# A prefix log-sum-exp whose last store is cut into eight transfers

## The chip, the cores and the metric

The kernel runs on one core of a Trainium2 chip. The metric is the device time of one execution in microseconds. A core has five compute engines with a queue each (PE, the matrix engine; DVE, the vector engine; ACT, the scalar engine; POOL; SP, which here only issues transfers) and 16 DMA engines that move data between the chip's memory (HBM) and the core's own memory, SBUF, which has 128 partitions.

## The reference

For x of shape (4, 4096, 4128) in float32, each of the 4 x 4128 columns gets a running log-sum-exp along the 4096 rows:

```python
out[:, 0, :] = x[:, 0, :].copy()
for t in range(1, S):
    mx = np.maximum(out[:, t - 1, :], x[:, t, :])
    out[:, t, :] = mx + np.log(np.exp(out[:, t - 1, :] - mx) + np.exp(x[:, t, :] - mx))
```

This is the logarithm of the running sum of exp(x). Every byte is read once and written once: 270.53 MB in and 270.53 MB out.

## The kernel before, in words

The 4096 rows of a batch are cut into steps of 128 x r rows, r being 2 or 3 (lists `begin`, `usual`, `final`; 49 steps in all). Partition p of a step's tile `x` holds r neighbouring rows, r x 4128 values in a row, so partition p's part is one contiguous run in HBM of 33,024 B (r = 2) or 49,536 B (r = 3). Four tiles (slots) rotate.

A step is one load (`Step.load`, line 88), then three chunks of 1376 columns, then one store (`Step.store`, line 91). A chunk takes the exponentials in place on ACT (line 102), adds the rows of a partition on DVE (lines 114 and 116), sums over the partitions below with a triangular matrix on PE (line 124), adds that base on DVE (lines 133, and 141 or, in the last step of a batch, 136) and takes the logarithms on ACT (lines 146 and 147).

The order of each engine's work is written out by hand in lists: `moves` for the transfers, `act`, `vec` and `pe`. All loads and stores are issued from SP in the order of `moves`, one transfer for a whole tile: four loads first, then store, load, store, load; the end is load, load and then the stores alone. Each transfer signals one of eight landing counters, which are taken in turn (numbers 100, 101, 105 to 110 in the trace). Each DMA engine that takes part in a transfer signals it once its share has landed, so the trace has 16 landings for each of the 98 transfers.

The very last store (step 48: the last of the last batch, r = 2) is issued once its three chunks' logarithms are done. Behind it on SP stand the load of a flag that says whether the fast form of the sum was safe (line 254), a branch, and the closing waits for all landing counters (line 308). The span ends when these are through.

Of the kernel before, what the change touches and what calls it, by code (L numbers as in the profile page):

```python
# [12 lines left out]
P = 128  # L13
# [8 lines left out]
def kernel(  # L22
# [5 lines left out]
    nc = tc.nc  # L28
    B, S, D = x.shape
# [16 lines left out]
        out=below, in_=below, pattern=[[1, P]], compare_op=ALU.is_ge,  # L46
# [5 lines left out]
        out=carried, in_=below, pattern=[[0, P]], compare_op=ALU.not_equal,  # L52
# [25 lines left out]
    class Step:  # L78
# [9 lines left out]
            nc.sync.dma_start(out=self.xt, in_=self.dram(x))  # L88

        def store(self):  # L90
            nc.sync.dma_start(out=self.dram(out), in_=self.xt)  # L91

    class Chunk:
        def __init__(self, step, c):
# [125 lines left out]
    done, at = set(), {e: 0 for e in lists}  # L220
    while any(at[e] < len(l) for e, l in lists.items()):
        before = len(done), sum(at.values())
        for e, l in lists.items():
            while at[e] < len(l):
                op = l[at[e]]
                if op[1] < n:
# [3 lines left out]
                    of = steps[op[1]]  # L230
# [8 lines left out]
        out=fits[:, :B * NC], in0=probe, scalar1=LARGE, scalar2=None, op0=ALU.is_le,  # L239
    )  # L240
    nc.vector.tensor_scalar(
        out=fits[0:1, B * NC:], in0=short, scalar1=0.0, scalar2=None, op0=ALU.is_le,
# [7 lines left out]
        out=flag, in0=good, scalar1=float(P), scalar2=None, op0=ALU.is_lt,  # L250
# [62 lines left out]
```

## Time and profile before

| | |
|---|---|
| median of 3 runs | 1261.32 us (1260.91 to 1261.74) |
| profiled execution | 1260.2 us, of it span 1258.4 us |
| DVE, ACT, PE busy | 956.2, 955.4, 602.4 us |
| DMA | 14,131 packets, 541.28 MB, 430 GB/s on the mean |
| loads | 30 of 6192 KB, 19 of 4128 KB |
| stores | 30 of 6192 KB, 19 of 4128 KB |
| last store issued, last landing, end of span | 1239.89, 1257.13, 1258.4 us |

The span is the time from the first to the last instruction of the profiled execution; the execution's own time is 1.8 us longer. A packet is what one DMA engine moves in one go, here the part of one partition, or the 4 bytes that signal a landing. A landing is the moment at which the counter is raised. The trace gives a packet's size, start and duration, not the number of the DMA engine that moved it.

### The profile page before, as it was taken

How to read it: one execution, taken by the hardware profiler on the slowest of the kernel's cores; microseconds unless marked ns; L12 is line 12 of the kernel's file. 1: busy time of each engine (PE TensorE's matmuls, PEld its weight loads, DVE VectorE, ACT ScalarE, POOL GpSimd, SP SyncE). 2: the span in 40 equal slices, each digit the busy share in tenths (PEclk: the TensorE clock that was granted, in tenths of full speed). 3: DMA queues.
4: the chain of work that ended last, by engine and by line, in shares of the span. 5: the costliest groups of instructions: out<-in, count | busy, mean ns of one | idle time of the engine just before them, and what ended most of it. 6: DMA issues, size and time to landing. Idle time of an engine off the chain costs nothing.

```text
span 1258.4 us, 3228 instructions
## 1 busy us (share of the span) xinstructions
PE 602.4 (48%) x884; PEld 233.1 (19%) x884; DVE 956.2 (76%) x548; ACT 955.4 (76%) x466; POOL 4.6 (0%) x14
## 2 busy tenths in 40 slices
PE   3654454453535455345364535634535553463361
PEld 1221121121212122112121212211211211121120
DVE  3997696795967699579596679957957976795792
ACT  6987687786976699578697668866968966896792
POOL 1000000000000000000000000000000000000000
PEclk9877776676677667666676666766766776676676
DMA  9999999999999999999999999999999999999998
GB/s 403 420 439 426 432 436 428 432 437 429 439 425 438 430 437 433 436 435 427 440 422 436 436 432 434 434 430 435 437 428 437 431 435 431 434 437 433 432 435 354
DMA packets 14131, 541.28 MB, mean 430 GB/s; under 512 B 1568, under 2 KB 1568, under 8 KB 1568
## 3 DMA queue, kind: packets, MB, share of 16 engines
q1 hardware_dynamic: 14112, 541.07, 99.6%
q8 instruction: 7, 0.11, 0.0%
q14 instruction: 12, 0.10, 0.0%
HBM read 270.53 MB, written 270.53 MB: 430 GB/s over the span
## 4 chain that ended last, share of the span: by engine, by line
DMA 69%; ACT 14%; DVE 13%; PE 1%; issue 1%; SPq 0%; ACTq 0%; DVEq 0%
DMA x<-in_x_dram 52%; DMA out_dram<-x 17%; ACT x L102 6%; DVE x L133 5%; ACT x L146 5%; DVE z L116 3%; ACT x L147 3%; DVE z L141 3%; DVE x L114 2%; PE p L124 1%; SPq L91 0%; DVE z L136 0%; ACTq L146 0%; ACTq L254 0%; SPq L88 0%
## 5 line engine op out<-in xcount | busy, mean ns | idle before, releaser
L124 PE MATMUL p<-z,carried 128*128 128x512 f32 (+1 forms) x810 | 551.8, 842 | 544.3 <-DVE z L116 544.3
L102 ACT ACTIVATE x<-x 128x4128 f32<-128x4128 f32 (+1 forms) x147 | 468.0, 3187 | 219.7 <-DMA x<-in_x_dram 219.7
L124 PEld LDWEIGHTS p<-z,carried 128*128 128x128 f32 x810 | 213.4, 280 | 882.2 <-DVE z L116 648.3
L133 DVE TENSOR_TENSOR x<-p,x 128x2752 f32<-128x2752 f32 (+1 forms) x147 | 361.9, 2462 | 6.2 <-PE p L124 6.2
L146 ACT ACTIVATE x<-x 128x2752 f32<-128x2752 f32 (+1 forms) x147 | 300.6, 2045 | 63.5 <-DVE z L141 58.5
L114 DVE TENSOR_TENSOR x<-x 128x1376 f32<-128x1376 f32 x90 | 142.9, 1588 | 216.5 <-ACT x L102 216.5
L116 DVE TENSOR_TENSOR z<-x 127x1376 f32<-127x1376 f32 x147 | 233.9, 1591 | 53.8 <-ACT x L102 49.4
L141 DVE TENSOR_TENSOR z<-x 128x1376 f32<-128x1376 f32 x135 | 215.0, 1592 | 4.6
L147 ACT ACTIVATE x<-z 128x1376 f32<-128x1376 f32 x147 | 196.0, 1334 | 0.0
L124 PE MATMUL p<-z,below 128*128 128x512 f32 (+1 forms) x72 | 50.4, 864 | 87.4 <-DVE z L116 87.4
L124 PEld LDWEIGHTS p<-z,below 128*128 128x128 f32 x72 | 19.6, 289 | 117.7 <-DVE z L116 78.8
L136 DVE CUSTOM_DVE_ANT_0 z<-x 128x1376 f32<-128x1376 f32 x12 | 19.1, 1592 | 0.4
L105 ACT ACTIVATE spare<-x,tiny 1x1376 f32<-1x1376 f32 x12 | 17.3, 1442 | 0.5
L69 POOL MEMSET z<- 128x1376 f32 x3 | 3.7, 1241 | 0.0
L105 ACT ACTIVATION_READ_ACCUMULATOR spare<-x,tiny 1x1 f32 x12 | 2.2, 186 | 0.0
L247 PE MATMUL good<-ones,low 128*1 128x1 f32 x2 | 0.2, 164 | 3.8 <-DVE low L245 3.8
L34 ACT ACT_TABLE_LOAD x1 | 1.3, 1283 | 0.8 <-PEq L297 0.8
L136 DVE DVE_READ_ACCUMULATOR2_ANT probe<- 128x1 f32 x12 | 1.0, 83 | 0.0
L247 PEld LDWEIGHTS good<-ones,low 128*1 128x1 f32 x2 | 0.1, 80 | 4.8 <-DVE low L245 4.8
L249 DVE TENSOR_SCALAR flag<-good 1x1 int32<-1x1 f32 x1 | 0.1, 148 | 0.3 <-PE good L247 0.3
L51 POOL TENSOR_SCALAR_AFFINE_SELECT carried<-below 128x128 f32<-128x128 f32 x1 | 0.3, 290 | 0.0
L45 POOL TENSOR_SCALAR_AFFINE_SELECT below<-below 128x128 f32<-128x128 f32 x1 | 0.3, 285 | 0.0
(13 smaller groups left out, 1.6 us busy)
## 6 DMA issues: line engine op xcount, KB each, us to landing
x<-in_x_dram SPq DMA_DIRECT2D x30, 6192.0 KB, 38.4
out_dram<-x SPq DMA_DIRECT2D x30, 6192.0 KB, 25.0
x<-in_x_dram SPq DMA_DIRECT2D x19, 4128.0 KB, 33.0
out_dram<-x SPq DMA_DIRECT2D x19, 4128.0 KB, 21.6
```

The lines of the kernel that those rows point to most:

```text
L34: nc.scalar.preload_act_table_set("natural_log_exp_and_others")
L69: nc.gpsimd.memset(t, 0.0)
L102: nc.scalar.activation(e, e, ACT.Exp)
L105: nc.scalar.activation(spare, t.xt[0:1, 0, self.cols], ACT.Relu, bias=tiny, scale=-1.0, accum_out=short[:, k:k + 1],)
L114: nc.vector.tensor_tensor(out=e[1], in0=e[0], in1=e[1], op=ALU.add)
L116: nc.vector.tensor_tensor(out=self.z[0:n], in0=e[r - 2][0:n], in1=e[r - 1][0:n], op=ALU.add,)
L124: nc.tensor.matmul(pt[:, a:b], lhsT=w, rhs=self.z[:, a:b], start=True, stop=True,)
L133: nc.vector.tensor_tensor(out=e, in0=base, in1=e, op=ALU.add)
L136: nc.vector.tensor_tensor_reduce(out=self.z, in0=ends[0], in1=ends[1], scale=1.0, scalar=0.0, op0=ALU.add, op1=ALU.add, accum_out=probe[:, ...
L141: nc.vector.tensor_tensor(out=self.z, in0=ends[0], in1=ends[1], op=ALU.add)
L146: nc.scalar.activation(e, e, ACT.Ln)
L147: nc.scalar.activation(t.xt[:, r - 1, self.cols], self.z, ACT.Ln)
```

## The change

Every store but the last stays as it is. The last one is issued as eight transfers, in this order: the first 112 partitions in full; the last 16 partitions without their last 59 columns; then these 59 columns of the 16 partitions in three strips of 17, 19 and 23 columns, each strip as two transfers (14 and 2, 12 and 4, 10 and 6 partitions). The eight together write the same bytes to the same places.

```diff
         def store(self):
-            nc.sync.dma_start(out=self.dram(out), in_=self.xt)
+            if self.last and self.b == B - 1:
+                self.pieces()
+            else:
+                nc.sync.dma_start(out=self.dram(out), in_=self.xt)
+
+        def pieces(self):
+            to = self.dram(out).rearrange("p j d -> p (j d)")
+            of = self.xt.rearrange("p j d -> p (j d)")
+            a, end = P - 16, self.r * D
+            parts = [(2, 17), (4, 19), (6, 23)]
+            at = end - sum(w for _, w in parts)
+            nc.sync.dma_start(out=to[:a], in_=of[:a])
+            nc.sync.dma_start(out=to[a:, :at], in_=of[a:, :at])
+            for k, w in parts:
+                cols = slice(at, at + w)
+                at += w
+                nc.sync.dma_start(out=to[a:P - k, cols], in_=of[a:P - k, cols])
+                nc.sync.dma_start(out=to[P - k:, cols], in_=of[P - k:, cols])
+            assert at == end
```

## The prediction

> **What bounds the kernel now.** I read the page's slices first, then its queue part, and then only the end of the span, because the change touches only the last store.
>
> Part 2 and part 3 of the page (slices of the span; queues):
>
> ```profile
> DMA  9999999999999999999999999999999999999998
> GB/s 403 420 439 426 432 436 428 432 437 429 439 425 438 430 437 433 436 435 427 440 422 436 436 432 434 434 430 435 437 428 437 431 435 431 434 437 433 432 435 354
> q1 hardware_dynamic: 14112, 541.07, 99.6%
> ```
>
> The 16 DMA engines are busy from end to end, all of it on one queue, so a microsecond of compute is worth nothing and bytes per microsecond are everything. Only the last slice drops, to 354 GB/s: a tail. The windows of the last 20 us (columns: stretch, its length, five engines busy, granted clock, DMA share, GB/s) show it:
>
> ```profile
> 1240.00:1245.00 5.00, 0.00 (x0) 0.00 (x0) 0.00 (x0) 0.00 (x0) 0.00 (x0) 0.50 0.99 429
> 1245.00:1250.00 5.00, 0.00 (x0) 0.00 (x0) 0.00 (x0) 0.00 (x0) 0.00 (x0) 0.50 1.01 436
> ...
> 1251.00:1252.00 1.00, 0.00 (x0) 0.00 (x0) 0.00 (x0) 0.00 (x0) 0.00 (x0) 0.50 0.65 272
> 1252.00:1253.00 1.00, 0.00 (x0) 0.00 (x0) 0.00 (x0) 0.00 (x0) 0.00 (x0) 0.50 0.54 231
> 1253.00:1254.00 1.00, 0.00 (x0) 0.00 (x0) 0.00 (x0) 0.00 (x0) 0.00 (x0) 0.50 0.31 132
> 1254.00:1255.00 1.00, 0.00 (x0) 0.00 (x0) 0.00 (x0) 0.00 (x0) 0.00 (x0) 0.50 0.31 132
> ...
> 1256.00:1257.00 1.00, 0.00 (x0) 0.00 (x0) 0.00 (x0) 0.00 (x0) 0.00 (x0) 0.50 0.00 0
> ```
>
> No compute is left after 1240; the engines run out of packets one after another from 1251 on. The packet records say why. The last store is 128 packets of 33,024 B, eight per engine, each 1.222 us (least 1.221): 27.0 GB/s per engine, and 16 at once make the 432 of the windows. Its 16 landings (one per engine) are at 1251.55 to 1253.69 for eleven engines and 1256.07 to 1257.13 for five. The store before it has the same spread, 1241.77 to 1247.12, so 5.35 us of lateness was gathered earlier in the kernel. The last packet ends at 1256.67, and the last wait on SP, which ends with the final landing, is the longest of its line:
>
> ```profile
> SPq L308 <- DMA out_dram<-x: 15.4, 2, 10.0
> ```
>
> From that landing to the end of the span is 1.3 us of closing barriers. So the end is the latest engine: its eight packets, then about 1.75 us.
>
> The issuing side, from the timeline of SP and from line 91 (count: least/median/most ns, first and last start):
>
> ```profile
> 1188.24 0.34 SPq L88 DMA_DIRECT2D x<-in_x_dram  x1
> 1189.55 50.68 SPq L91 DMA_DIRECT2D out_dram<-x  x4
> ```
> ```profile
> L91 SPq DMA_DIRECT2D out_dram<-x x49: 332/332/347, 38.0 to 1239.9; - x49
> ```
>
> The last store is issued at 1239.89 and its first packet starts at 1241.38, when the queue gets to it.
>
> **The change, part by part.** One issue of 128 packets becomes eight issues of 112 + 16 + 14 + 2 + 12 + 4 + 10 + 6 = 176 packets. The bytes are the same.
>
> *Issuing.* Seven more issues on SP. The four loads that open the kernel are issued back to back at 0.80, 1.24, 1.71 and 2.18, so 0.47 us each: 7 x 0.47 = 3.3 us, the last at about 1243.2. The 16-partition store is needed when the earliest engine has done its seven packets, 1241.38 + 7 x 1.222 = 1249.9: covered by over 6 us. SP rotates eight landing counters. The last store uses 101, the new ones the next seven, the eighth piece that of the store issued at 1228.04, which lands at 1247.12. If SP waits for it, that piece goes out at 1247.2; from issue to first packet the opening load took 1.0 us (0.80 to 1.81): 1248.2, still before 1249.9. Behind that wait on SP stand the load of the flag and the branch (1240.28 to 1241.7, 1.4 us): done by 1249.1, and nobody needs SP before the landing at 1257. Cost 0; without the queue's backlog it would be the 3.3 us. POOL's queue is empty, and the closing waits already poll all eight counters, so no wait is added there.
>
> *Small transfers.* 48 packets of 68, 76 and 92 B, and seven more sets of landing writes (4 B, 0.009 us each). The 16 large last packets lose 236 B, 0.009 us. An engine has at most six small packets. Nothing of that size is in the trace: below, 0.009 us each, 0.05 us; above, each pair made to wait for its own write to land, by the last store's 0.46 us from packet end to landing (1256.67 to 1257.13), 6 x 0.46 = 2.8 us. I take 0.1, because landing writes in mid-stream hold up nothing: data packets follow them within 0.01 us. Below nothing is excluded: no byte goes away.
>
> *The new deal of partitions.* This is the term that matters. In every transfer of the trace 128 partitions go to 16 engines, eight each, in one fixed deal, so each engine always has the same eighth of partitions to itself. 112 and 16 partitions are dealt seven and one to an engine: still eight packets each, but now other partitions. If an engine's own 27.0 GB/s is the limit, the cost is 0. If the way out of SBUF for a group of eight partitions is the limit, also 27.0 GB/s, engines that meet in one group halve each other. The trace can't part the two, because no two engines ever share a group; the bounds come from the packet row.
> - The 16 last partitions: evenly spread over 16 ways, 0; all in two groups of eight, eight packets each where there was one, 7 x 1.222 = 8.56 us. I take four per way, 3 x 1.222 = 3.67, the whole number of packets closest to the middle (4.28).
> - The 112: at each of seven steps 16 engines read from at most 14 groups, so some double up. Least, 14 doublings shared by 16 engines, about one each, 1.22; most, the same pairs double at every step, 8.56 us. The engines are 5.35 us out of step, over four packets, so pairs form and dissolve: I take half of seven, rounded down, three, 3.67.
> A gain is bounded too: were the 16 dealt to early engines alone, the late five would be spared a packet, -1.22.
>
> The Trainium skill ("SBUF — State Buffer", section on the DMA port swizzle) speaks against the change: four neighbouring partitions and the four 32 further on share one of 16 ports, and a transfer over 16 partitions was measured there at 104 GB/s. By that rate the 16 partitions (524,608 B) would take an estimated 5.0 us where one packet time is 1.22, which makes that term +3.8 in place of 3.67. No run here shows it; the 27.0 GB/s per engine agrees with its 27.2 per port.
>
> Sum: 3.67 + 3.67 + 0.1 = +7.4 us. The profiled execution is 1260.2 us (span 1258.4 and 1.8 around it), 1.1 under the median of 1261.32, inside the habit of this kernel (1260.91 to 1261.74 timed). Profiled: 1267.6; median: 1268.7.
>
> **The rivals.** What a measurement of this kernel can tell from no change is about 0.2%, 2.5 us.
> - *No sharing*: the engine is the limit, and eight packets are eight packets wherever they come from. For it: 1.221 to 1.222 us in loads and stores alike, and an instruction fetch on the same engine just adds (1.53 = 1.222 + 0.309). Against: nothing, since the two limits have one value here. Time 1261.3 + 0.1 = 1261.4.
> - *Harder sharing*: the last 16 through two groups, +8.56, and the 112 at +6.1 (five of seven): 1276. It needs partitions grouped in plain runs of eight; but then a plain deal of eight is the only one that gives today's full rate.
> - *Serial small pieces*: no sharing, but each waits for its landing: +2.8, 1264.1. It counts only if the six-piece engines are among the late five; an early engine has up to 5.35 us to spare.
> - *Faster*: the lateness itself shrinks. A longer instruction stream moves the fetches: the late stretch holds one of 16,384 B at 1215.3 (0.89 us) and two of 8,192 B at 1205.5 and 1251.2 (0.31 each). If all three moved from late to early engines, -1.5, 1259.8; it decides only from 2.5 us, so two of the earlier large fetches (0.91 to 0.99 us each) must move too: 1257.9. The packet at 1251.51 that took 1.49 us shows that a fetch does hit the tail.
> - *Not what it says*: rows of 8,197 elements could be cut into more packets (8,197 = 7 x 1,171), 112 in place of 16; at 0.009 us a packet less than 0.1 us per engine. Price nil.
>
> **How the numbers follow.** Sharing as summed 0.62, no sharing 0.21 (1260.7 to 1262), harder sharing 0.08, serial pieces 0.05, faster 0.04. I lean to sharing because 16 engines at exactly 27.0 GB/s with no spread, in both directions, look like fixed lanes rather than engines competing for memory. Predicted is the likeliest, 1268.7. Its own range: one packet per step at least (1.22 + 1.22 + 0.1: 1263.9) to five and three (6.1 + 3.67 + 0.1: 1271.2) and a little over for the order of the late engines. The range takes in no sharing without its lowest part and stops short of hard sharing: 1261.0 to 1274.0; below it lie the fast case and some of the undisturbed one (0.10), above it hard sharing (0.08). Slower by over 0.2%: 0.62 + 0.08 + 0.04 = 0.74 (a fifth of the serial case stays within); same: 0.22; faster: 0.04.
>
> **What would show it.** Right: in the last 20 us packets of 33,024 B that take 1.8 to 2.5 us, the DMA share still full but GB/s falling below 400 from about 1242, sixteen packets of 32,788 B taking 2.4 to 5 us, the last landing near 1264. Wrong, if these stay at 1.22 and the last landing is at 1257: then the engine, not its partitions, sets the rate. The small transfers: 48 packets under 100 B of about 0.01 us; gaps of 0.4 us between them would be the serial case. SP's issues should lie 0.4 us apart from 1239.9, all but the last before 1244. If the spread of landings of the store before (5.35 us) changes, the lateness moved, and part of the difference isn't the deal.

## The result, and the profile after

The changed kernel takes 1268.88 us (median of 5; 1265.94 to 1269.98) against 1261.08 us (median of 5): +7.8 us, a ratio of 1.0057 with a 95% interval of 1.0042 to 1.0072. Its profiled execution is 1268.88 us, with a span of 1267.1. The kernel before scatters by 0.8 us, the changed one by 4 us.

The slices of the span after show where the time went: nowhere but in the last slice, which falls to 245 GB/s.

```profile
DMA  9999999999999999999999999999999999999996
GB/s 400 422 436 422 438 436 432 434 433 427 439 424 441 431 429 437 438 432 434 428 439 426 441 434 425 440 425 433 434 441 434 434 429 432 433 433 443 427 430 245
```

The windows of the changed kernel's last 25 us (columns: stretch, length, busy time of PE, PEld, DVE, ACT, POOL, granted clock, DMA share, GB/s; a packet's time and bytes are counted where it starts, so a share can exceed 1):

```profile
1240.00:1245.00 5.00, 0.00 (x0) 0.00 (x0) 0.00 (x0) 0.33 (x1) 0.00 (x0) 0.50 1.03 423
1245.00:1250.00 5.00, 0.00 (x0) 0.00 (x0) 0.00 (x0) 0.00 (x0) 0.00 (x0) 0.50 1.08 363
1250.00:1255.00 5.00, 0.00 (x0) 0.00 (x0) 0.00 (x0) 0.00 (x0) 0.00 (x0) 0.50 1.04 297
1255.00:1260.00 5.00, 0.00 (x0) 0.00 (x0) 0.00 (x0) 0.00 (x0) 0.00 (x0) 0.50 0.17 66
1260.00:1265.00 5.00, 0.00 (x0) 0.00 (x0) 0.00 (x0) 0.00 (x0) 0.00 (x0) 0.50 0.05 22
```

This is what to look for when a transfer is slow without being idle: between 1245 and 1255 the engines are as busy as ever (1.08, 1.04), yet move 363 and 297 GB/s where the kernel before moved 436 between 1245 and 1250. The packets got longer. Of the 177 large packets that start after 1240, 40 take over 1.4 us and the longest 4.95 us; before, one of 169 did (the 1.49 us beside an instruction fetch). Seven of the sixteen packets of 32,788 B still take 1.21 to 1.24 us, the others 1.57 to 4.95. From 1255 on the window is nearly empty (0.17): a few engines are left, and in the end one. The last landing comes at 1265.79 instead of 1257.13.

That engine can be followed packet by packet, since each of its packets starts where the one before ended. Its last packets of the store *before* the changed one took 2.75 and 4.72 us instead of 1.22, so that store's last landing slipped from 1247.12 to 1252.83. Its seven packets of the 112 took 2.19, 2.07, 1.65 and then 1.22 to 1.24 four times, the packet of the 16 took 1.21, and five small ones followed. So 5 of the 8.7 us between the two profiles' last landings were lost before it had begun the changed store.

The timeline of SP after:

```profile
1240.36 0.35 SPq L102 DMA_DIRECT2D out_dram<-x  x1
1240.75 0.44 SPq L103 DMA_DIRECT2D out_dram<-x  x1
1241.24 1.03 SPq L107 DMA_DIRECT2D out_dram<-x  x1
1242.31 1.74 SPq L108 DMA_DIRECT2D out_dram<-x  x1
1244.10 1.03 SPq L107 DMA_DIRECT2D out_dram<-x  x1
1245.17 3.70 SPq L108 DMA_DIRECT2D out_dram<-x  x1
1248.92 3.05 SPq L107 DMA_DIRECT2D out_dram<-x  x1
1252.84 1.61 SPq L108 DMA_DIRECT2D out_dram<-x  x1
```

The two large issues cost 0.35 and 0.44 us, the six small ones 1.03 to 3.70: 12.2 us of SP in place of the 2.8 that the prediction gave them. The last goes out at 1252.84. That is still ahead of the engine that sets the end, but it made a rival worth testing: is it the issuing that costs?

### The profile page after: what moved, and what is told of

It reads as the page before. It is cut to its first block, busy times and chain, and to the rows that moved or that the text cites. A ratio compares the mean times of both kernels' runs of the same rounds, so it can differ in the third digit from the quotient of the medians.

```text
span 1267.1 us, 3235 instructions
## 1 busy us (share of the span) xinstructions
PE 608.2 (48%) x884; PEld 234.8 (19%) x884; DVE 956.0 (75%) x548; ACT 955.4 (75%) x466; POOL 4.6 (0%) x14
## 4 chain that ended last, share of the span: by engine, by line
DMA 69%; ACT 14%; DVE 12%; PE 1%; issue 1%; SPq 0%; ACTq 0%; DVEq 0%
DMA x<-in_x_dram 52%; DMA out_dram<-x 17%; ACT x L120 6%; DVE x L151 5%; ACT x L164 5%; DVE z L134 3%; ACT x L165 3%; DVE z L159 3%; DVE x L132 1%; PE p L142 1%; SPq L94 0%; DVE z L154 0%; ACTq L164 0%; ACTq L272 0%; SPq L88 0%
## 5 line engine op out<-in xcount | busy, mean ns | idle before, releaser
L142 PE MATMUL p<-z,carried 128*128 128x512 f32 (+1 forms) x810 | 558.0, 850 | 541.1 <-DVE z L134 541.1
```

The source lines that it names most:

```text
L142: nc.tensor.matmul(pt[:, a:b], lhsT=w, rhs=self.z[:, a:b], start=True, stop=True,)
```

## The experiments

All times are medians, and each change is against the kernel before timed along with it on the same chip (1260.95, 1260.70 or 1260.79 us). "Deal" is which partitions of a transfer go to which DMA engine; a "way" is the path between a group of partitions and the DMA engines.

| last store as | us | change | ratio, 95% interval |
|---|---|---|---|
| 112 + 16, no strips | 1267.02 | +6.1 | 1.0045 (1.0031 to 1.0059) |
| 128 less 59 columns, then the strips | 1261.92 | +1.0 | 1.0008 (0.9999 to 1.0017) |
| eight column pieces of all 128 | 1261.63 | +0.7 | 1.0006 (0.9997 to 1.0015) |
| 64 + 64 | 1268.18 | +7.2 | 1.0057 (1.0042 to 1.0073) |
| 8 x 16 neighbours | 1270.62 | +9.9 | 1.0077 (1.0060 to 1.0094) |
| 8 x 16, every eighth | 1268.22 | +7.5 | 1.0072 (1.0053 to 1.0091) |
| first load as 16 + 112 | 1269.21 (one run) | +8.5 | - |
| 112 alone | 1265.93 | +5.1 | 1.0034 (1.0021 to 1.0046) |
| 128, then 16 again | 1267.20 | +6.4 | 1.0049 (1.0032 to 1.0066) |
| 16 + 112 | 1266.20 | +5.4 | 1.0040 (1.0026 to 1.0055) |

### The deal or the issues

Four runs part the deal of partitions from the number and smallness of the transfers. First the two large transfers without the strips (this edit and the next are shown against the changed kernel, the later ones against the kernel before; `...` marks lines left out):

```diff
-            parts = [(2, 17), (4, 19), (6, 23)]
...
             nc.sync.dma_start(out=to[:a], in_=of[:a])
-            nc.sync.dma_start(out=to[a:, :at], in_=of[a:, :at])
-            for k, w in parts:
...
+            nc.sync.dma_start(out=to[a:], in_=of[a:])
```

> The last store as 112 and 16 whole partitions, without the strips. Deal theory (engines that read from one group of eight partitions halve each other): nearly the whole loss stays, 1266 to 1270 us (+5 to +9), less about 0.9 us, which is what the five small landings of the last engine took after its large one in the changed kernel (1264.88 to 1265.79). Rival, the issuing theory (the six small issues took 1.0 to 3.7 us each on SP instead of 0.33, and hold up what follows): the loss goes, 1261 to 1262.

Measured: 1267.02 us, +6.1. The loss stays, with two issues instead of eight. The counterpart keeps the old deal and has the small transfers:

```diff
-            nc.sync.dma_start(out=to[:a], in_=of[:a])
-            nc.sync.dma_start(out=to[a:, :at], in_=of[a:, :at])
+            nc.sync.dma_start(out=to[:, :at], in_=of[:, :at])
+            nc.sync.dma_start(out=to[:a, at:], in_=of[:a, at:])
```

> The store keeps all 128 partitions in one transfer (8,197 columns), the last 59 columns follow as one transfer of 112 partitions and the six small ones. Deal theory: large packets stay at 1.22 us, only small landings are added, 1261 to 1263 us (+0.2 to +1.5). Issuing theory: +5 to +8, 1266 to 1269. The three strip widths also tell which engines are late.

Measured: 1261.92 us, +1.0; the interval just takes in no change. Five of its six small issues take about 1 us each too (0.95 to 1.03; the last, 0.27), so slow issues alone don't make the loss. The windows of this run:

```profile
1245.00:1250.00 5.00, 0.00 (x0) 0.00 (x0) 0.00 (x0) 0.00 (x0) 0.00 (x0) 0.50 1.02 440
1250.00:1255.00 5.00, 0.00 (x0) 0.00 (x0) 0.00 (x0) 0.00 (x0) 0.00 (x0) 0.50 0.59 242
1255.00:1260.00 5.00, 0.00 (x0) 0.00 (x0) 0.00 (x0) 0.00 (x0) 0.00 (x0) 0.50 0.06 21
```

440 GB/s to 1250, then the tail of the kernel before: no packet is stretched. As many issues as the change has, all with 128 partitions:

```diff
+            w = self.r * D // 8
+            for k in range(8):
+                cols = slice(k * w, (k + 1) * w)
+                nc.sync.dma_start(out=to[:, cols], in_=of[:, cols])
```

> The last store as eight transfers of 128 partitions and 1,032 columns each: as many issues as the change has, the old deal of partitions. Deal theory: 1261 to 1262.5 us, packets of 4,128 B at 27 GB/s. If the number of transfers is what costs: +3 to +8, 1264 to 1269.

Measured: 1261.63 us, +0.7, not told from zero. The pieces need only the chunks that they cover, so the first went out at 1230.14 already; with the queue full that bought nothing. One piece took about 1.30 us per engine (landings 1.30 us apart), eight 10.4, against 9.78 for eight packets of 33,024 B: 0.6 us, about what was measured. And two large halves:

```diff
+            a = P // 2
+            nc.sync.dma_start(out=to[:a], in_=of[:a])
+            nc.sync.dma_start(out=to[a:], in_=of[a:])
```

> The last store as two transfers of 64 partitions, four to an engine. Deal theory: each half comes out of half of the groups, so two engines share each group at any time; between them the transfers overlap because the engines are 5 us out of step: +6 to +9.5 us, 1267 to 1271. Issuing theory, or an engine that is its own limit: +0 to +0.5, 1261 to 1262.

Measured: 1268.18 us, +7.2: two issues of four packets per engine cost as much as the whole change. Its windows:

```profile
1240.00:1245.00 5.00, 0.00 (x0) 0.00 (x0) 0.00 (x0) 0.00 (x0) 0.00 (x0) 0.50 1.06 396
1245.00:1250.00 5.00, 0.00 (x0) 0.00 (x0) 0.00 (x0) 0.00 (x0) 0.00 (x0) 0.50 1.02 277
1250.00:1255.00 5.00, 0.00 (x0) 0.00 (x0) 0.00 (x0) 0.00 (x0) 0.00 (x0) 0.50 0.96 272
```

Busy and slow again, and from the first packet on. Issuing is out: what the lossy runs share is that their large transfers take fewer than 128 partitions.

### Which partitions share a way

> The last store as eight transfers of 16 neighbouring partitions, one to an engine. If ways out are shared by four neighbours together with the four 32 further on, each transfer comes through four ways: +12 to +18 us, 1273 to 1279. If they are shared by plain runs of eight, each comes through two: +23 to +32, 1284 to 1293. No sharing: +0 to +1.

```diff
+            for k in range(0, P, 16):
+                nc.sync.dma_start(out=to[k:k + 16], in_=of[k:k + 16])
```

> The last store as eight transfers of 16 partitions, each every eighth one, so engine e always reads from the run of eight 8e to 8e+7. If ways out are shared by plain runs of eight, nobody meets anybody: +0 to +1 us, 1261 to 1262. If they are shared by four neighbours together with the four 32 further on, two engines meet in every packet: +7 to +13, 1268 to 1274. No sharing: +0 to +1, the same as plain runs, which the run with neighbours then tells apart.

```diff
+            for k in range(8):
+                nc.sync.dma_start(out=to[k:P:8], in_=of[k:P:8])
```

Measured: 16 neighbours +9.9 us, every eighth +7.5. The second is the clean one. If each plain run of eight partitions had its own way, engine e would have had run e to itself and nothing would have been lost. It lost 7.5 us, most of its packets settled at 2.42 to 2.59 us, which is two engines per way, and its GB/s at half:

```profile
1250.00:1255.00 5.00, 0.00 (x0) 0.00 (x0) 0.00 (x0) 0.00 (x0) 0.00 (x0) 0.50 0.69 178
1255.00:1260.00 5.00, 0.00 (x0) 0.00 (x0) 0.00 (x0) 0.00 (x0) 0.00 (x0) 0.50 1.01 225
```

Plain runs are excluded, if the 16 partitions of a transfer go to the 16 engines in the same order each time. Ways shared by four neighbours and the four 32 further on fit: partitions 8e and 8e + 32 belong to engines e and e + 4, which then meet. The runs don't single out the 32, though: four neighbours with the four 16 further on would make two engines meet here and give 16 neighbours four ways as well. The neighbours' run missed its range of +12 to +18 on the low side; probably because consecutive transfers use different ways and the engines, out of step, work in two or three of them at once, which was not tried apart. It is far from the +23 to +32 of plain runs.

The Trainium skill ("SBUF — State Buffer", section on the DMA port swizzle) has this grouping as its 16 ports, four neighbours with the four 32 further on, and the runs agree. It was only one of two groupings in the prediction's bounds.

Which end of the transfer is shared was not tried apart: in every run partition p also has its own place in HBM, so a new deal changes both ends. For the SBUF side speak the packet times at about two and four times 1.222 us, in loads and stores alike, and that in the kernel before tiles whose partitions lie 49,536 B apart in HBM run at the rate of those 33,024 B apart (1.829 and 1.222 us a packet, 27 GB/s per engine in both).

### The disputed packets by themselves

```diff
         def load(self):
-            nc.sync.dma_start(out=self.xt, in_=self.dram(x))
+            if self.n == 0:
+                a = P - 16
...
+                nc.sync.dma_start(out=to[a:], in_=of[a:])
+                nc.sync.dma_start(out=to[:a], in_=of[:a])
+            else:
+                nc.sync.dma_start(out=self.xt, in_=self.dram(x))
```

> The very first load, into an empty queue, as 16 partitions (112 to 127) and then 112. The disputed packets alone: 16 engines start together and nothing else is in flight. The first packets took 1.8 to 2.1 us in the kernel before. Sharing of four ways: about 4.9 us each. Two ways: about 9.8 us. No sharing: 1.8 to 2.1 us. The first load then ends 4 to 8 us later under sharing.

The windows of the first microseconds of this run, which hold the start of the 16 packets:

```profile
1.00:3.00 2.00, 0.00 (x0) 0.00 (x0) 0.00 (x0) 1.08 (x1) 1.96 (x7) 1.00 1.87 264
3.00:5.00 2.00, 0.00 (x0) 0.00 (x0) 0.00 (x0) 0.00 (x0) 2.00 (x3) 1.00 0.00 0
```

and of the kernel before:

```profile
1.00:3.00 2.00, 0.00 (x0) 0.00 (x0) 0.00 (x0) 1.08 (x1) 1.96 (x7) 1.00 0.94 264
3.00:5.00 2.00, 0.00 (x0) 0.00 (x0) 0.00 (x0) 0.00 (x0) 2.00 (x3) 1.00 0.73 314
```

Both start 16 packets in the first window (264 GB/s x 2 us = 528 KB). A share of 1.87 x 2 us x 16 engines / 16 packets is 3.7 us a packet; before it is 1.9. From the first start (1.82) to the last end (6.71) are 4.89 us, four times 1.222, as four ways for 16 partitions would give. Each packet (3.36 to 4.43) is shorter than that, probably because not all start together; and since the opening packets of the kernel before took 1.8 to 2.1 us where 1.222 is usual, this is a rough measure. The 112 behind them run at 2.2 us a packet (the median; 1.6 to 3.0), and the load lands at 22.62 instead of 13.05: 9.6 us later, more than the 4 to 8 expected. So loads suffer as stores do, and engines in step with each other don't escape: at the kernel's start they are within 0.6 us.

A store of the 16 alone came out of a run that was meant for something else:

```diff
+            a = P - 16
+            nc.sync.dma_start(out=to, in_=of)
+            nc.sync.dma_start(out=to[a:], in_=of[a:])
```

> All 128 partitions in one transfer as before, and then the last 16 partitions once more, the same bytes to the same place: one packet more for each engine, through four ways. If the deal of the 112 carries the loss: the early engines wait in the tail while the late ones still work, and the end moves by the late engines' own packet and little else: 1262 to 1263.5 us. If the tail costs its 3.67 us on top of the packet: about 1265.8 us.

Measured: 1267.20 us, +6.4, outside both expectations, because SP waited for the first store's landing before it wrote the same place again. Its longest wait, its timeline and its window:

```profile
SPq L101 <- DMA out_dram<-x: 16.0, 1, 16.0
```
```profile
1240.38 0.33 SPq L100 DMA_DIRECT2D out_dram<-x  x1
1258.01 0.35 SPq L101 DMA_DIRECT2D out_dram<-x  x1
```
```profile
1258.00:1260.00 2.00, 0.00 (x0) 0.00 (x0) 0.00 (x0) 0.00 (x0) 0.00 (x0) 0.50 2.45 264
```

As a test of the tail it says nothing. As a measurement of 16 stored packets with nothing beside them it is the best of the study: 2.45 x 2 us x 16 / 16 = 4.9 us a packet (4.72 to 5.08), against 1.22 for an engine that has its way to itself. 528,384 B from 1258.87 to 1264.10 are 101 GB/s.

### Which of the two terms

The prediction gave 3.67 us to the 112 and 3.67 to the last 16.

```diff
+            a = P - 16
+            nc.sync.dma_start(out=to[:a], in_=of[:a])
```

> Only the 112 partitions are stored; the last 16 of the last step are left out of the output. If the deal of the 112 carries the loss and the 16 cost their own packet time, the end comes one packet (1.22 us) before that of the 112 and 16 without strips: about 1265.8 us (1264.5 to 1267). If the loss is half and half, as the prediction split it, 3.67 + 1.22 go with the 16: about 1262.1 us (1261.3 to 1263.2).

```diff
+            a = P - 16
+            nc.sync.dma_start(out=to[a:], in_=of[a:])
+            nc.sync.dma_start(out=to[:a], in_=of[:a])
```

> The same two transfers in the other order, the last 16 partitions first. If the deal of the 112 carries the loss: the whole loss stays, 1265.5 to 1270 us. If half of it comes from the 16 partitions being last, that half goes: about 1264.5 us.

Measured: 112 alone 1265.93 us, +5.1, though one packet per engine is missing: in the range for a loss that the 112 carry. 16 first, then 112: 1266.20 us, +5.4; the median is in the range for the whole loss, but the interval (1264.1 to 1267.7) reaches down to the 1264.5 of the other case, so it is no verdict by itself. From 112 alone to 112 + 16 the loss grows by 0.9 us (5.1 to 6.1), no more than the packet that was missing (1.22). So the 112 carry the loss: 5.14 + 1.22 = 6.4 us by the medians (3.9 to 7.0 by the interval of the ratio), and the 16, though they take up to 5.06 us on the early engines in the run without strips, cost the end only their own packet.

In that run of the 112 alone the engine that ends last shows where it is lost. Its last two packets of the store before took 4.34 and 4.55 us, 6.4 over their 2.44; of its seven of the 112 five took 1.22 and two 1.46 and 1.64. That store's last landing is at 1254.07 in this run, 1250.61 with 112 + 16, 1251.24 with 16 + 112 and 1252.83 in the changed kernel; before it is 1247.12, and 1248.43 with the strips alone. The reading that fits: the early engines begin the new deal while a late one still reads its own group in the old deal; packets of 3.6 to 3.7 times 1.22 us would mean that two or three of them come through its way with it, so the engine that is already last is held up. The trace doesn't number the engines, so who met whom isn't shown. Nor is it the whole story: with 64 + 64 the store before landed at 1248.98, hardly late, and the loss was as large.

## Why the prediction was right

Forecast: 1268.7 us, slower; measured: 1268.88. The mechanism, engines that share a way, held; the total came out too, but inside it two terms were mis-sized in opposite directions.

- *What bounds the kernel* held: only the last slice changed, and the end is the latest engine.
- *No sharing* (1261.4 us) is out: the store alone shows 4.9 us where 1.22 was possible, and every run whose large transfers of the last store take fewer than 128 partitions lost 5 us or more (medians). The 1.53 us quoted for it is a sum: in the trace a packet of 33,024 B right behind a fetch took 1.47 to 1.83 us itself, not 1.222.
- *The last 16 partitions* was a term that failed. Four per way was right as a packet time (4.9 us), but the term asked what it adds to the end, and on the engine that sets the end it adds only its own packet, which was there before. The early engines have over 5 us to spare, and that is where the long packets fell. Taken 3.67; measured about 0 (0.9 less 1.22, within the scatter).
- *The 112* failed the other way. It was counted as seven steps of the changed store, three doubled. Measured 6.4 us, between its bounds of 1.22 and 8.56, and much of it lies where the prediction did not look: on the late engine's last packets of the store before, whose landing slipped by 5.7 us (4.4 against the run with the strips alone). The prediction said what to read from that (a change there means that lateness moved); it moved because of the deal. In the first load, where the engines start together, the packets of the 112 took 2.2 us at the median, 1.8 times 1.222; whether fewer steps double when the engines are out of step was not tried apart.
- *Small transfers*: taken 0.1, and the bound above was 2.8. The packets take 0.009 to 0.012 us, about as said, but the last engine's small landings come about 0.18 us apart, from 1264.88 to 1265.79: 0.9 us. The run with the strips alone gives +1.0, the difference between the change and 112 + 16 is 1.7 with overlapping intervals. "Landing writes in mid-stream hold up nothing" was read from a stream of 33,024 B packets; behind 68 B packets a landing can't hide.
- *Issuing* was rightly 0, by a wrong working: six issues took 1.03 to 3.70 us where 0.47 was taken, the last started at 1252.84 instead of 1247.2, and its wait for a landing was longer since the landing itself was late. The flag and the branch were done by 1256.5, seven us before the landing that SP waited for. The cover was large enough for an error of over 5 us.
- *Harder sharing* was excluded by the run with every eighth partition, *faster* by the loss itself. The serial case is a small part of the result, 0.9 of its 2.8 us. *Not what it says*: the 16 rows went as one packet each.

The total was right to 0.2 us with terms wrong by 3.67 and 2.7, and a third, the small transfers, by about 0.8: that is luck within the range. The prediction's own range for this case, 1263.9 to 1271.2, is the honest statement; the five timings of the changed kernel alone run from 1265.94 to 1269.98.

No run points to a version faster than the kernel before. The 5 us between its early and its late engines stay on the table.

## What to carry to other kernels

Keep the deal of 128 partitions for every large transfer of a kernel that is bound by DMA, loads and stores alike: splitting by columns cost 0.7 us here, not told from zero, splitting by partitions 5 to 10. A busy share of 1 with falling GB/s and packets of the same size shows that packets take longer; here the cause was engines that share a way. When a new pattern enters a full queue, look at what is still in flight ahead of it: the latest engine of the transfer before can pay the most.

## What the runs showed of the hardware that was not expected

- The issue of a transfer can take SP several microseconds. With 16-partition transfers one behind the other it was 0.34 and 0.41 us for the first two and 2.05 to 5.18 for the next six; with small strips behind a 128-partition store about 1.0 for five of six; with column eighths 0.33 to 0.72. In these runs it grew when transfers with few packets piled up behind a full queue. What SP waits for inside the issue was not tried and stays open.
- The six small transfers landed on 14, 2, 12, 4, 10 and 6 engines, so at least two engines moved none of their packets. The Trainium skill ("DMA: Bandwidth & Descriptors", section on why a DMA increments its semaphore by 16) says that a transfer runs on the lowest-numbered engines, their count being the largest number up to 16 that divides its partitions; the counts agree, though the trace doesn't number the engines. Here the latest engine of the changed kernel had five small packets and the one before it four, by their landings.
